# Where the up projection's first quad takes its weights from, and the y products of the SSD scan in one piece

## The chip, the cores and the metric

The kernel runs on one core of a Trainium2 chip. The metric is the device time of one execution in microseconds (us). All data are float32; most matrix products run in float32r, as three products of a high and a low part of each operand, so that the sum is close to float32.

## The reference

One decoder layer on 512 tokens of width 1024, cut to what the change touches:

```
h    = rms_norm(x) @ w_in                      # z, x/B/C, dt, q, k, v, f
y    = ssd_mixer(...)                          # 16 heads in 2 groups, chunks of 128 tokens
       y_diag = (C B^T * decay) @ (x dt)       # inside a chunk
       y_off  = (C exp(a_cs)) @ state          # from the chunks before it
       y      = rms_norm((y_diag + y_off + D x) * silu(z))   # per group of 512
x    = x + concat(y, fox_attention(...)) @ w_out
hf   = rms_norm(x)
u    = causal_conv3(hf @ w_up)                 # 1024 -> 5632, halves gate and value
out  = x + (silu(gate) * value) @ w_down       # 2816 -> 1024
```

## The kernel before, in words

**Splitting.** A weight block of 128 x 1024 comes by DMA into a raw tile, ScalarE (ACT) copies it into a float32r tile `wh`, VectorE (DVE) puts the rest `wl = raw - wh` into a second tile, and TensorE (PE) multiplies. `mm3` (line 110 is its matmul) issues the three products high by high, high by low, low by high for one block of 128 columns. Raw tiles `wraw` stand in a ring of three, the pairs `wh`, `wl` in another ring of three, beside a spare pair and, in the up stage, a far pair.

**Order.** A scheduler works out one static order for each engine, from the program's order, priorities (`urgent()`), explicit "issue after" edges and its own estimates of time. Each engine runs its order strictly: an instruction whose operand is late holds all behind it. Tiles of a pool are handed out in rotation as the scheduler places the work, so which of the three PSUM banks of a pool a sum gets also depends on the order.

**The SSD scan** (`ssd_scan`, two groups of eight heads) goes through four chunks of 128 tokens. For each, `side_by_side` issues 16 matmuls of 64 columns each as PE sees them (8 instructions in the order lists), two heads next to each other in the two column halves of the array: first the chunk's own product (`sc` by `x_tok`), then, from the second chunk on, the product with the state (`ce` by `state`) into the same bank `y`. Between the two, `norm_sum` puts one tiny matmul `ss`, the sum of squares of an earlier chunk. `x_tok` of the first chunk is filled by `to_tokens`, two heads at a time, as the projections that feed it come in: each pair of matmuls may start as soon as its two heads are there. PE meanwhile streams the 128 x 512 products of the projections (`g`, `pw`, `po`).

**The up projection** is done with one level of a Strassen-like scheme (seven products instead of eight) on eleven quads of four weight blocks, named B11, B12, B21, B22. Quad 0 is done plainly (`plain`): `weights` loads and splits its four blocks, `tokens(0)` multiplies with the first half of the tokens, `tokens(1)` with the second. Sums Z take B12 and B22, sums G take B11 and B21. Quad 0 starts while the last of the output projection (`po`, w7) and the second norm (`up_norm`, `up_turn`, transposes `hT`) are still running; the normed tokens stand in `uh` (high) and `ul` (low). All four raw blocks use the ring `wraw`, and B11 and B21 are split into the ring of three pairs, whose tiles the output projection's last weights still hold.

The later quads keep running sums of weight blocks: a tile `T` (named Ta, Tb; two of them in pool `ptt`, one in `pu`) receives a block, is split, and then another block is added into it by an accumulating DMA that GpSimd (POOL) issues (line 965, `more`). For quad 1 this is a chain of steps: n0's split, then an added block, n2's split, another added block, n3's split. SyncE (SP) issues the plain loads.

Of the kernel before, what the change touches and what calls it, by code (L numbers as in the profile page):

```python
# [8 lines left out]
F32 = mybir.dt.float32  # L9
F32R = mybir.dt.float32r  # L10
# [5 lines left out]
P = 128  # L16
# [17 lines left out]
LINE = 64  # L34
# [5 lines left out]
def tile_hybrid_layer(  # L40
# [18 lines left out]
    nc = tc.nc  # L59
# [329 lines left out]
    def ssd_proj(g):  # L389
        x_tok = [pss.tile([P, 512], F32, tag="x_tok", name="x_tok", bufs=7) for _ in range(NTB)]  # L390
        bT = pss.tile([P, SEQ], F32, tag="bT", name="bT", bufs=2)
        cT = pss.tile([P, SEQ], F32, tag="cT", name="cT", bufs=2)
        b_tok = pss.tile([P, NTB, P], F32, tag="b_tok", name="b_tok", bufs=2)
        gz = pss.tile([P, 4, SEQ], F32, tag="gz", name="gz", bufs=2)
        dx = pa.tile([P, 4, SEQ], F32, tag="v", name="dx", bufs=2)

        def to_tokens(j, src):
            t = obank("xT")
            for c in range(NTB):
                tc.keep_in_program_order(  # L400
                    pe.transpose(t[:, c * P : (c + 1) * P], src[:, c * P : (c + 1) * P], ident)
                )
            tv = t.rearrange("p (c f) -> p c f", c=NTB)
            if j < 8:
                jj = j - 4 * g
                for c in range(NTB):
                    for i in range(2):
                        h = 2 * jj + i
                        act.activation(
                            x_tok[c][:, h * HD : (h + 1) * HD], tv[:, c, i * HD : (i + 1) * HD], AF.Copy,  # L410
                            scale=tokS[:, 0, c, g * HPG + h : g * HPG + h + 1],
                        )
            else:
                act.copy(b_tok, tv)

        late = []
        for n, j in enumerate([8 + g, 10 + g] + list(range(4 * g, 4 * g + 4))):
            o = early.pop(j, None) or feature_tile(wxbc[j])
            if n > 3:
                to_tokens(*late.pop(0))  # L420
            xp = tmp("t", "xp")
            dve.tensor_mul(xp, o, R)
            dst = bT if j in (8, 9) else cT if j > 9 else tmp("t", "xs")
            cw = C_SCW + 4 * j
            act.activation(
                dst, xp, AF.Identity, scale=half_w[:, cw + 3 : cw + 4], bias=half_w[:, C_SCB + j : C_SCB + j + 1]
            )
            for s in range(1, 4):
                dve.scalar_tensor_tensor(
                    out=dst[:, s:], in0=xp[:, : SEQ - s], scalar=half_w[:, cw + 3 - s : cw + 4 - s], in1=dst[:, s:],  # L430
                    op0=ALU.mult, op1=ALU.add,
                )
            act.activation(xp, dst, AF.Tanh)
            dve.scalar_tensor_tensor(out=dst, in0=xp, scalar=1.0, in1=dst, op0=ALU.add, op1=ALU.mult)
            if j < 8:
                act.activation(dx[:, j - 4 * g, :], dst, AF.Copy, scale=pc[:, C_D + j : C_D + j + 1])
            if j < 10:
                late.append((j, dst))

        for j in range(4):  # L440
            o = feature_tile(wz[4 * g + j])
            if late:
                to_tokens(*late.pop(0))
            z = gz[:, j, :]
            th = tmp("t", "th")
            dve.tensor_mul(z, o, R)
            act.activation(th, z, AF.Tanh, scale=0.5)
            dve.scalar_tensor_tensor(out=z, in0=th, scalar=1.0, in1=z, op0=ALU.add, op1=ALU.mult)
        return x_tok, bT, cT, b_tok, gz, dx
# [4 lines left out]
    def per_head(ap):  # L454
        return ap[:, :, None].broadcast_to([P, HPG, HD])

    squares = []

    def norm_sum(after):
        g, c, t = squares.pop(0)  # L460
# [5 lines left out]
    def ssd_scan(g, x_tok, bT, cT, b_tok, gz, dx):  # L466
# [27 lines left out]
            dve.tensor_mul(sc, sc, cb[:, None, :P].broadcast_to([P, HPG, P]))  # L494
            return sc, ce, dte

        def side_by_side(o, w, m, start, stop):
            for j in range(4):
                for i, rows in ((1, HI), (0, LO)):
                    h = 2 * j + i  # L500
                    ins = pe.matmul(  # L501
                        o[rows, j * P : (j + 1) * P], w[:, h * HD : (h + 1) * HD], m[:, h, :],
                        start=start and j == 0, stop=stop and j == 3, skip_group_check=True,
                    )
                    if (j, i) != (0, 1):
                        tc.keep_in_program_order(ins)
            return ins

        def chunk(c, state, sc, ce, dte):
            s = slice(c * P, (c + 1) * P)  # L510
            o = mbank("y")
            own = side_by_side(o, x_tok[c], sc, True, c == 0)
            if c > 0:
                norm_sum(own)
                side_by_side(o, state, ce, False, True)
            if c < NTB - 1:
                xt = heads(x_tok[c])
                dve.tensor_mul(xt, xt, per_head(dte[:, 0, :]))
# [294 lines left out]
    def up_operand(n):  # L813
        return (oh[:, n], ol[:, n]) if n < 4 else (sh[:, n - 4], sl[:, n - 4])
# [126 lines left out]

    halfway, last_product, last_pool = [None], [None], [None]

    def product(w, n, o, part, first=False, last=True):
        h, l = w
        ah, al = up_operand(n) if n is not None else (gh, gl)
        for p in range(2):
            for k in range(4):
                c = slice(p * 512 + k * P, p * 512 + (k + 1) * P)
                ins = mm3(  # L950
                    o[:, p, part], h[:, c], l[:, c], ah[:, k], al[:, k], first and k == 0, last and k == 3, grouped=False
                )
            if p == 0:
                halfway[0] = ins
        last_product[0] = ins
# [309 lines left out]
    def spare():  # L1265
        return [pa.tile([P, 1024], F32R, tag=t, name=t, bufs=1) for t in ("wh", "wl")]

    def plain(q):
        u = quads[q]
        u.ws, u.halfway = [], []  # L1270

        def weights(quarter, where=None):
            r = wp.tile([P, 1024], F32, tag="wraw", name="wraw", bufs=3)
            nc.sync.dma_start(r, wup[quarter, q])
            u.ws.append(split_up(r, where))

        def tokens(half):
            for n, (name, rows) in enumerate((("Z", 0), ("Z", 1), ("G", 0), ("G", 1))):
                o = getattr(u, name)
                op = ((0, 1), (None, 2))[half][rows]  # L1280
                product(u.ws[n], op, o, (H1, H2)[half], rows == 0, rows == 1)
                u.halfway.append(halfway[0])

        return weights, tokens
# [15 lines left out]
    quads[0].Z = two_banks("Z", "Z")  # L1300
    sum_banks.close()
    up_banks["G"] = ctx.enter_context(tc.tile_pool(name="pq", bufs=2, space=PSUM, reuse_waits="tile"))
    weights(B11)
    with urgent():
        normed = up_norm(NTB - 1)
        act.activation(warm[:, 0:1], ss[:, NTB - 1 : NTB], AF.Silu)
# [14 lines left out]
    n2(1)  # L1321
    n5(1)
    four = [[wp.tile([P, 1024], F32R, tag=t, name=t, bufs=3) for t in ("wh", "wl")] for _ in range(3)]

    four.append([pu.tile([P, 1024 + LINE], F32R, tag=t, name=t)[:, LINE // 4 : 1024 + LINE // 4] for t in ("wh", "wl")])
    pairs.update(n2=four[0], n4=four[3], n1=four[1], n5=four[2])
    n0_weights(2)
    n3_weights(1)
# [297 lines left out]
```

## Time and profile before

| | us |
|---|---|
| runs (three) | 768.78, 770.18, 770.66 |
| median | 770.18 |
| profiled execution | 768.29 |
| its span | 766.5 |
| PE busy | 757.8 (99%) |
| DVE busy | 604.2 (79%) |
| ACT busy | 487.9 (64%) |

A row of the timeline has the start in us from the span's start, the duration in us, engine, source line, operation, output and inputs, shapes, the number of instructions merged, and in brackets the idle time before it and what ended it. Matmul rows overlap: a 128 x 512 product lasts 0.39 us and the next starts 0.23 us after it, so PE's pace is read from starts, and PE's idle time in brackets is shorter than the delay of the start.

### The profile page before, as it was taken

The page shows a single profiled execution, that of the slowest core. Times are in us where ns is not written, and L with a number is a line of the kernel's source. Part 1 is how long each engine was busy: PE and PEld are TensorE (multiplying, and loading weights), DVE is VectorE, ACT ScalarE, POOL GpSimd, SP SyncE. Part 2 cuts the span into 40 slices and gives each one's busy share as a digit, 9 for nine tenths or more (in the row PEclk, how much of TensorE's full clock was granted, in tenths as well). Part 3 has the DMA queues.
Part 4 walks back from the last instruction along what each step waited for, and adds up shares of the span by engine and source line. Part 5 has one row for each costly group of instructions (what it writes and reads, how often), then busy time and mean ns, then how long its engine had stood idle before and what let it go on. Part 6 is the DMA issues. An engine that isn't in the chain of part 4 may idle for free.

```text
span 766.5 us, 12541 instructions
## 1 busy us (share of the span) xinstructions
PE 757.8 (99%) x4647; PEld 650.8 (85%) x4647; DVE 604.2 (79%) x965; ACT 487.9 (64%) x870; POOL 200.7 (26%) x250
## 2 busy tenths in 40 slices
PE   9999999999999999999999999999999999999997
PEld 7888778787788778787777799999999999888786
DVE  5896789588568667488894887888888888998785
ACT  7655767664388667695673665766666666665461
POOL 0001013344253562235200001333333333213120
PEclk9999999999999999999999999999999999999999
DMA  9524223142154243334322317888888888589993
GB/s 342 181 99 143 90 103 132 62 138 90 49 192 128 65 152 96 111 126 123 83 83 83 110 56 150 198 195 195 195 193 195 193 195 192 152 236 209 240 192 99
DMA packets 35005, 112.39 MB, mean 147 GB/s; under 512 B 4160, under 2 KB 5248, under 8 KB 34944
## 3 DMA queue, kind: packets, MB, share of 16 engines
q1 hardware_dynamic: 24176, 74.89, 28.6%
q0 software_dynamic: 10336, 36.18, 26.1%
q8 instruction: 36, 0.59, 0.3%
q10 hardware_dynamic: 432, 0.52, 0.2%
q14 instruction: 25, 0.20, 0.1%
HBM read 105.71 MB, written 2.20 MB: 141 GB/s over the span
## 4 chain that ended last, share of the span: by engine, by line
PE 91%; issue 3%; DMA 2%; DVE 1%; POOL 1%; ACT 0%; SPq 0%; DVEq 0%; POOLq 0%; ACTq 0%
PE G L110 19%; PE pw L110 17%; PE g L110 13%; PE po L110 11%; PE Z L110 11%; PE Y L110 3%; PE o L681 2%; PE pT L671 2%; PE X L110 2%; PE y L501 2%; PE j L110 1%; PE S L648 1%; PE S L649 1%; POOL T L1204 1%; DMA T<-in_wdown_dram 1%
## 5 line engine op out<-in xcount | busy, mean ns | idle before, releaser
L110 PE MATMUL pw<-wh,xl 128*128 128x512 f32 x192 | 76.0, 396 | 0.0
L110 PE MATMUL pw<-wh,xh 128*128 128x512 f32 x192 | 75.8, 397 | 0.0
L110 PE MATMUL pw<-wl,xh 128*128 128x512 f32 x192 | 75.5, 393 | 0.0
L97 DVE TENSOR_TENSOR wl<-wraw,wh 128x1024 fp32r<-128x1024 f32 x51 | 64.0, 1255 | 13.1 <-ACT wh L96 12.7
L110 PE MATMUL G<-uh,wh 128*128 128x256 f32 x264 | 72.6, 277 | 0.9 <-DVE x L278 0.9
L110 PE MATMUL G<-ul,wh 128*128 128x256 f32 x264 | 72.5, 276 | 0.0
L110 PE MATMUL G<-uh,wl 128*128 128x256 f32 x264 | 71.6, 277 | 0.6 <-DVE wl L920 0.6
L96 ACT CAST wh<-wraw 128x1024 fp32r<-128x1024 f32 x51 | 53.5, 1051 | 19.0 <-PE pw L110 8.4
L110 PE MATMUL g<-xh,wl 128*128 128x512 f32 x144 | 56.8, 394 | 0.0
L110 PE MATMUL g<-xh,wh 128*128 128x512 f32 x144 | 56.8, 394 | 0.0
L110 PE MATMUL g<-xl,wh 128*128 128x512 f32 x144 | 56.7, 394 | 0.0
L965 POOL DMA_DIRECT2D Ta<-in_wup_dram x30 | 26.3, 875 | 113.1 <-DVE wl L920 113.1
L1215 ACT CAST wh<-T 128x1024 fp32r<-128x1024 f32 (+1 forms) x32 | 31.5, 985 | 33.4 <-DMA T<-in_wdown_dram 18.7
L920 DVE TENSOR_TENSOR wl<-Ta,wh 128x1024 fp32r<-128x1024 f32 x40 | 48.7, 1218 | 2.8 <-ACT wh L920 2.8
L110 PEld LDWEIGHTS G<-uh,wh 128*128 128x128 f32 x264 | 49.6, 188 | 1.3 <-ACT wh L920 1.3
L110 PEld LDWEIGHTS G<-ul,wh 128*128 128x128 f32 x264 | 49.6, 188 | 0.0
L110 PEld LDWEIGHTS G<-uh,wl 128*128 128x128 f32 x264 | 48.9, 188 | 0.8 <-DVE wl L920 0.8
L650 DVE CUSTOM_DVE_ANT_0 prob<-S,prob 128x128 f32<-128x128 f32 (+1 forms) x64 | 29.9, 486 | 23.8 <-PE S L649 22.1
L1215 DVE TENSOR_TENSOR wl<-T,wh 128x1024 fp32r<-128x1024 f32 (+1 forms) x32 | 36.4, 1137 | 13.4 <-ACT wh L1215 13.4
L920 ACT CAST wh<-Ta 128x1024 fp32r<-128x1024 f32 x40 | 42.1, 1053 | 6.3 <-DMA Ta<-in_wup_dram 4.3
L654 ACT ACTIVATE prob<-prob,nm 128x128 f32<-128x128 f32 (+1 forms) x64 | 35.7, 559 | 15.6 <-DVE nm L650 15.4
L110 PE MATMUL G<-sh,wh 128*128 128x256 f32 x160 | 44.2, 276 | 0.0
(296 smaller groups left out, 2415.4 us busy)
## 6 DMA issues: line engine op xcount, KB each, us to landing
Ta<-in_wup_dram POOLq DMA_DIRECT2D x30, 512.0 KB, 5.5
T<-in_wdown_dram POOLq DMA_DIRECT2D x20, 512.0 KB, 7.4
wraw<-in_wqk_dram SPq DMA_DIRECT2D x16, 512.0 KB, 3.4
wraw<-in_wout_dram SPq DMA_DIRECT2D x16, 512.0 KB, 3.3
wraw<-in_wup_dram SPq DMA_DIRECT2D x14, 512.0 KB, 4.9
wraw<-in_wxbc_dram SPq DMA_DIRECT2D x11, 512.0 KB, 3.3
Ta<-in_wup_dram SPq DMA_DIRECT2D x10, 512.0 KB, 7.0
Tb<-in_wup_dram SPq DMA_DIRECT2D x10, 512.0 KB, 6.4
```

The source lines that it names most:

```text
L96: act.copy(h, r)
L97: dve.tensor_tensor(out=l, in0=r, in1=raw(h), op=ALU.subtract)
L110: ins = pe.matmul(o, a, b, start=start and n == 0, stop=stop and n == 2, **kw)
L501: ins = pe.matmul(o[rows, j * P : (j + 1) * P], w[:, h * HD : (h + 1) * HD], m[:, h, :], start=start and j == 0, stop=stop and j == 3, ski ...
L648: pe.matmul(sps[:, :n], qst, ks[:, 0, :n], start=True, stop=False)
L650: dve.tensor_tensor_reduce(out=p, in0=sps[:, :n], in1=p, scale=-1.0, scalar=-NEG, op0=ALU.add, op1=ALU.min, accum_out=nm[:, qb : qb + 1],)
L654: act.activation(p, p, AF.Exp, scale=-1.0, bias=nm[:, qb : qb + 1], accum_out=sm[:, qb : qb + 1])
L671: pe.transpose(t[:, w : w + P], prob[:, o : o + P], ident)
L681: ins = pe.matmul(o[rows, kb * P :], v[:, kb, (2 * pair + i) % 8, :], pt[:, w : w + SEQ - kb * P], start=kb == 0, stop=kb == NTB - 1, skip ...
L920: ordered(act.copy(h, r), lambda: dve.tensor_tensor(out=l, in0=r, in1=raw(h), op=SUB))
L965: last_more[0] = nc.gpsimd.dma_start(t, wup[quarter, q], accum_op=ALU.add)
L1215: ordered(act.copy(hs, src[:, :n]), lambda: dve.tensor_tensor(out=ls, in0=src[:, :n], in1=raw(hs), op=SUB))
```

## The change

It has four parts.

1. The first matmul of the first chunk's own y product waits for the last of the copies into that chunk's `x_tok` (`copied[0]`); the others follow it in program order, as they did.
2. `norm_sum` stands behind the state's product instead of between the two y products.
3. Raw blocks B11 and B21 of quad 0 are loaded into the two `T` tiles of pool `ptt`, which hold the running sums of quads 2 and 3 later, at the time that `plain(0)` is set up. B11's split goes into the far pair in pool `pu` (the new `far_pair`, called a second time where the far pair was made before).
4. Quad 0's first G product, B11 with the first half of the tokens, runs through `low_last`: eight matmuls of high weights by high tokens, eight of low weights by high tokens, eight of high weights by low tokens.

```diff
                     for i in range(2):
                         h = 2 * jj + i
-                        act.activation(
+                        copied[c] = act.activation(
                             x_tok[c][:, h * HD : (h + 1) * HD], tv[:, c, i * HD : (i + 1) * HD], AF.Copy,
...
-        def side_by_side(o, w, m, start, stop):
+        def side_by_side(o, w, m, start, stop, whole=None):
...
                     if (j, i) != (0, 1):
                         tc.keep_in_program_order(ins)
+                    elif whole is not None:
+                        dep = mybir.DependencyInfo(mybir.DependencyClass.Sync, mybir.DependencyReason.DATA)
+                        tc.add_manual_dep(ins.ins, whole.ins.name, dep, reason="issue_after")
             return ins
...
-            own = side_by_side(o, x_tok[c], sc, True, c == 0)
+
+            side_by_side(o, x_tok[c], sc, True, c == 0, copied[c] if c == 0 else None)
             if c > 0:
-                norm_sum(own)
-                side_by_side(o, state, ce, False, True)
+                norm_sum(side_by_side(o, state, ce, False, True))
...
+    def low_last(w, n, o, part):
+
+        (h, l), (ah, al) = w, up_operand(n)
+        for a, b in ((h, ah), (l, ah), (h, al)):
+            for p in range(2):
+                for k in range(4):
+                    c = slice(p * 512 + k * P, p * 512 + (k + 1) * P)
+                    last_product[0] = halfway[0] = pe.matmul(
+                        o[:, p, part], a[:, c], b[:, k], start=a is h and b is ah and k == 0, stop=False, skip_group_check=True
+                    )
...
+    def far_pair():
+
+        return [pu.tile([P, 1024 + LINE], F32R, tag=t, name=t)[:, LINE // 4 : 1024 + LINE // 4] for t in ("wh", "wl")]
...
+        def load_rows(quarter, pool_, tag, bufs):
+            r = pool_.tile([P, 1024], F32, tag=tag, name=tag, bufs=bufs)
+            nc.sync.dma_start(r, wup[quarter, q])
+            return r
+
+        held = {n: load_rows(n, ptt, "T", 2) for n in (B11, B21)}
...
         def weights(quarter, where=None):
-            r = wp.tile([P, 1024], F32, tag="wraw", name="wraw", bufs=3)
-            nc.sync.dma_start(r, wup[quarter, q])
+            r = held[quarter] if quarter in held else load_rows(quarter, wp, "wraw", 3)
             u.ws.append(split_up(r, where))
...
-                product(u.ws[n], op, o, (H1, H2)[half], rows == 0, rows == 1)
+                if half == 0 and n == 2:
+                    low_last(u.ws[n], op, o, H1)
+                else:
+                    product(u.ws[n], op, o, (H1, H2)[half], rows == 0, rows == 1)
...
-    weights(B11)
+    weights(B11, far_pair())
...
-    four.append([pu.tile([P, 1024 + LINE], F32R, tag=t, name=t)[:, LINE // 4 : 1024 + LINE // 4] for t in ("wh", "wl")])
+    four.append(far_pair())
```

The change moves instructions on every engine, since the scheduler works out the order anew. Three places matter for what follows. Source lines of the changed kernel are up to 27 higher: the matmul of y is still line 501, the up split is 920 before and 923 now, `low_last` is 954.

**PE, the scan's second chunk of group 0**, where the two y products and the tiny `ss` stand in the stream of projections `g`. Before:

```order
L110 MATMUL g<-xh,wl 128x512
L501 MATMUL y<-sc,x_tok 64x128 x8
L463 MATMUL ss<-ones,yt 128x1
L501 MATMUL y<-ce,state 64x128 x8
L110 MATMUL g<-xh,wh 128x512
```

Now:

```order
L110 MATMUL g<-xl,wh 128x512
L501 MATMUL y<-sc,x_tok 64x128 x8
L501 MATMUL y<-ce,state 64x128 x8
L463 MATMUL ss<-ones,yt 128x1
L401 MATMUL xT<-ident,xs 128x128 x4
```

The two y products now follow each other in this chunk and in the five others that have a state; in the first chunk of group 0 the four separate pieces (`x2` each, with some 20 projections from one to the next) have become one `x8` where the last piece stood.

**PE and DVE at the start of quad 0**, with the semaphores that an instruction waits for. `x_85` is the residual, to which the output projection's sums `po` are added. PE before:

```order
L110 MATMUL po<-wh,mfl 128x512
L110 MATMUL G<-uh,wh 128x256 [waits DVE_49,Activation_49]
L110 MATMUL G<-ul,wh 128x256
L110 MATMUL G<-uh,wl 128x256 [waits DVE_49]
L110 MATMUL G<-uh,wh 128x256
```

PE now:

```order
L110 MATMUL po<-wh,mfl 128x512
L954 MATMUL G<-uh,wh 128x256 [waits DVE_49,Activation_49]
L954 MATMUL G<-uh,wh 128x256 x7
L954 MATMUL G<-uh,wl 128x256 x8
L954 MATMUL G<-ul,wh 128x256 [waits DVE_49]
L954 MATMUL G<-ul,wh 128x256 x7
L110 MATMUL G<-uh,wh 128x256 [waits Activation_49]
L110 MATMUL G<-ul,wh 128x256
L864 MATMUL hT<-ident,xw 128x128 [waits DVE_49,PE_49,Activation_49]
```

DVE before:

```order
L920 TENSOR_TENSOR wl<-wraw,wh 128x1024
L866 TENSOR_TENSOR ul<-one,uh 128x8x128
L278 TENSOR_TENSOR x_85<-po,x_85 128x512 x2
L866 TENSOR_TENSOR ul<-one,uh 128x8x128
L278 TENSOR_TENSOR x_85<-po,x_85 128x512
L125 TENSOR_SCALAR misc<-misc 128x1
L278 TENSOR_TENSOR x_85<-po,x_85 128x512
L920 TENSOR_TENSOR wl<-wraw,wh 128x1024
L849 SCALAR_TENSOR_TENSOR xw<-x_85,misc,nw 128x512 x2
```

DVE now:

```order
L923 TENSOR_TENSOR wl<-wraw,wh 128x1024
L923 TENSOR_TENSOR wl<-T,wh 128x1024
L278 TENSOR_TENSOR x_85<-po,x_85 128x512
L869 TENSOR_TENSOR ul<-one,uh 128x8x128
L278 TENSOR_TENSOR x_85<-po,x_85 128x512 x2
L869 TENSOR_TENSOR ul<-one,uh 128x8x128
L278 TENSOR_TENSOR x_85<-po,x_85 128x512
L125 TENSOR_SCALAR misc<-misc 128x1
L852 SCALAR_TENSOR_TENSOR xw<-x_85,misc,nw 128x512 x2
```

B11's low split has moved from behind the last addition to `x_85` to ahead of the last four, and the second `ul` has moved behind one more addition. On PE the wait for `wl` is gone, and one for `ul` has come, 16 matmuls later.

**ACT and PE in quad 1**, at the third and fourth split from Ta, with `z_4808` the kept sum that n5's product overwrites in Z. ACT before:

```order
L959 COPY y_4746<-G 128x512
L920 CAST wh<-Ta 128x1024
L959 COPY z_4808<-Z 128x512
L920 CAST wh<-Ta 128x1024
L1147 ACTIVATE ua<-ua 128x512 x2
```

ACT now:

```order
L973 COPY y_4746<-G 128x512
L923 CAST wh<-Ta 128x1024 x2
L973 COPY z_4808<-Z 128x512
L1161 ACTIVATE ua<-ua 128x512
L923 CAST wh<-Tb 128x1024
```

PE before, n5's product (Z) behind n1's (G, with `uh`), and n3's (G, with `sh`) only after the 24 of n5:

```order
L110 MATMUL G<-uh,wh 128x256
L110 MATMUL G<-ul,wh 128x256
L110 MATMUL G<-uh,wl 128x256
L110 MATMUL Z<-sh,wh 128x256
L110 MATMUL Z<-sl,wh 128x256
```

PE now:

```order
L110 MATMUL G<-uh,wl 128x256
L110 MATMUL G<-sh,wh 128x256
L110 MATMUL G<-sl,wh 128x256
L110 MATMUL Z<-sh,wh 128x256
L110 MATMUL Z<-sl,wh 128x256
```

The first two matmuls of n3 now stand ahead of n5's 24, and ACT's cast of n3's weights stands ahead of its copy of `z_4808`.

More of the change, by code (lines that the diff above doesn't have):

```diff
@@ L455, in per_head @@
         return ap[:, :, None].broadcast_to([P, HPG, HD])
-    squares = []
+    squares, copied = [], {}
     def norm_sum(after):
```

## The prediction

> **What bounds the kernel.** I read the page first (busy times, then the chain of work that ended last), then PE's waits, then PE's timeline at the places that the change touches.
>
> ```profile
> span 766.5 us, 12541 instructions
> PE 757.8 (99%) x4647; PEld 650.8 (85%) x4647; DVE 604.2 (79%) x965; ACT 487.9 (64%) x870; POOL 200.7 (26%) x250
> PE 91%; issue 3%; DMA 2%; DVE 1%; POOL 1%; ACT 0%; SPq 0%; DVEq 0%; POOLq 0%; ACTq 0%
> PE G L110 <- DVE x L278: 0.9, 1, 0.9
> PE G L110 <- DVE wl L920: 0.6, 1, 0.6
> ```
>
> PE is busy for 99% of the span and carries 91% of the chain. So there are two ways to gain: take out one of its few waits, or make its own stream shorter. The last two rows are the two waits at the start of quad 0, and no row of PE's waits names `y`: the scattered pieces never waited. What they cost must stand in PE's pace around them.
>
> **The change part by part.** *The four pieces of the first y product become one.* The first fence has the first piece, the second a whole product in group 1.
>
> ```profile
> 80.84 0.39 PE L110 MATMUL g<-xh,wh 128*128 128x512 f32 x1
> 81.16 0.44 PE L501 MATMUL y<-sc,x_tok 128*64 128x128 f32 x4
> 81.53 0.50 PE L110 MATMUL g<-xl,wh 128*128 128x512 f32 x1
> 81.87 0.39 PE L110 MATMUL g<-xh,wl 128*128 128x512 f32 x1
> ```
>
> ```profile
> 165.45 0.39 PE L110 MATMUL po<-wl,msh 128*128 128x512 f32 x1
> 165.68 0.39 PE L110 MATMUL po<-wh,msl 128*128 128x512 f32 x1
> 165.99 1.09 PE L501 MATMUL y<-sc,x_tok 128*64 128x128 f32 x16
> 167.02 0.50 PE L110 MATMUL po<-wh,msh 128*128 128x512 f32 x1
> 167.35 0.40 PE L110 MATMUL po<-wl,msh 128*128 128x512 f32 x1
> ```
>
> The undisturbed step of the stream is 165.68 - 165.45 = 0.23. From the last product before the piece to the second after it, 81.87 - 80.84 = 1.03; two steps would be 0.46, so a piece of 4 adds 0.57. The whole block adds 167.35 - 165.68 - 0.46 = 1.21. Four pieces at 0.57 make 2.28, one block 1.21: **-1.1**. The added wait for the last copy costs nothing where the block stands, at the old last piece, which needed that copy too and did not wait. Behind it in PE's queue are projections alone. If every piece had cost its share of a whole block, the gain would be 0; that is the lower end.
>
> *The tiny `ss` behind both y products, in six chunks.*
>
> ```profile
> 114.26 0.39 PE L110 MATMUL g<-xh,wl 128*128 128x512 f32 x1
> 114.58 1.09 PE L501 MATMUL y<-sc,x_tok 128*64 128x128 f32 x16
> 115.60 0.38 PE L463 MATMUL ss<-ones,yt 128*128 128x1 f32 x2
> 115.91 1.09 PE L501 MATMUL y<-ce,state 128*64 128x128 f32 x16
> 116.94 0.50 PE L110 MATMUL g<-xh,wh 128*128 128x512 f32 x1
> 117.27 0.40 PE L110 MATMUL g<-xl,wh 128*128 128x512 f32 x1
> ```
>
> ```profile
> 241.73 0.40 PE L110 MATMUL pw<-wh,xh 128*128 128x512 f32 x1
> 241.96 0.28 PE L463 MATMUL ss<-ones,yt 128*128 128x1 f32 x2
> 242.10 0.48 PE L110 MATMUL pw<-wl,xh 128*128 128x512 f32 x1
> 242.41 0.40 PE L110 MATMUL pw<-wh,xl 128*128 128x512 f32 x1
> ```
>
> Before, the group takes 117.27 - 114.26 = 3.01. After: 0.32 into the first y, 1.02 for it (114.58 to 115.60), the second y right behind. From the rows above, 12 more matmuls cost 1.21 - 0.57 = 0.64, so 16 more cost 0.85; I take 0.90. Then `ss`, and out of it 0.14 + 0.31 (241.96 to 242.41). The sum is 2.69, a gain of 0.32 a chunk. No row shows 32 y matmuls in one run. The other end: two whole blocks (1.21 each) and a lone `ss` (242.41 - 241.73 - 0.46 = 0.22) add 2.64 where the group before adds 3.01 - 0.46 = 2.55, a loss of 0.09. I take 0.32, since a run that goes on is what the 4 against 16 show: **-1.9** for six, between -1.9 and +0.5. The Trainium skill ("TensorEngine Tiling (Array Packing)", Key Properties) says that a change of tiling mode drains the array; y runs in tiles of 128 x 64, `ss` does not. By that rule each chunk loses two switches and the gain stands at its upper end; without it, at the lower. The rows above (0.37 for 4 matmuls, 1.03 for 16) side with the rule.
>
> Counted over the order lists, two other small groups on PE have also merged with neighbours, at about 0.2 each by the lone `ss`: **-0.4**, with 1 either way, since the whole mixer is ordered anew.
>
> *Quad 0's start.*
>
> ```profile
> 438.55 0.39 PE L110 MATMUL po<-wh,mfl 128*128 128x512 f32 x1
> 439.81 0.36 PE L110 MATMUL G<-uh,wh 128*128 128x256 f32 x1 [0.88 <-DVE x L278]
> 440.00 0.28 PE L110 MATMUL G<-ul,wh 128*128 128x256 f32 x1
> 440.85 0.39 PE L110 MATMUL G<-uh,wl 128*128 128x256 f32 x1 [0.57 <-DVE wl L920]
> ```
>
> ```profile
> 437.00 1.22 DVE L866 TENSOR_TENSOR ul<-one,uh 128x1024 fp32r<-128x1024 f32 x1
> 438.97 0.69 DVE L278 TENSOR_TENSOR x<-po,x 128x512 f32<-128x512 f32 x1
> 439.58 1.22 DVE L920 TENSOR_TENSOR wl<-wraw,wh 128x1024 fp32r<-128x1024 f32 x1
> 442.85 1.42 DVE L849 SCALAR_TENSOR_TENSOR xw<-x,misc,nw 128x512 f32<-128x512 f32 x2 [0.66 <-POOL misc L126]
> ```
>
> The second wait (0.57) is for B11's low split, which the third DVE row makes behind the last residual addition. It now stands ahead of four additions and has the far pair free, so **-0.6** (up to 0.7 by starts). The first wait (0.88) is for that last addition itself, at 438.97 + 0.69 = 439.66: G's bank was its bank. The change says nothing of banks, but the new order does: PE now waits for DVE a second time at `ul`, which stands *ahead* of the last addition; a first wait for the last addition would have covered it. So G has another bank and the 0.88 goes too: **-0.9**, or 0 if I misread it. What is late next: DVE has 1.22 more ahead, and one addition (about 0.6) more ahead of the second `ul`, which then ends near 437.00 + 1.22 + 1.22 + 0.6 = 440.0; PE needs it after 16 matmuls of 0.115 from 438.78, at 440.6. That holds. Then the transposes `hT` of the third token block need `xw`: by the same delay it starts about 0.6 later than before, near 441.3, and is half done (0.7) at 442.0, while PE is there after 26 matmuls, at 441.8: **+0.3** with the semaphore.
>
> *Quad 1.*
>
> ```profile
> 471.21 0.58 ACT L959 COPY z<-Z 128x512 f32<-128x512 f32 x1
> 472.78 1.05 ACT L920 CAST wh<-Ta 128x1024 fp32r<-128x1024 f32 x1 [1.00 <-DMA Ta<-in_wup_dram]
> ```
>
> ```profile
> 472.89 0.28 PE L110 MATMUL Z<-sh,wh 128*128 128x256 f32 x1
> 473.00 0.28 PE L110 MATMUL Z<-sl,wh 128*128 128x256 f32 x1
> ```
>
> Now n3's first two matmuls stand where Z<-sh stood, at 472.89, and need the cast that ends at 472.78 + 1.05 = 473.83. Both ends of this gap hang on PE's own earlier products (through n0's pair, its split and two accumulating transfers), so both move by the same amount and the gap stays: **+1.0**. Then Z<-sh needs the copy of `z_4808`, which has moved behind that cast: it ends near 473.74 + 0.58 = 474.32, PE is there at 473.88 + 0.23 = 474.11: **+0.25**. Between 0, if the transfers land a microsecond sooner, and the slower rival below.
>
> **The sum:** -1.1 - 1.9 - 0.4 - 0.6 - 0.9 + 0.3 + 1.25 = -3.35. On the profiled execution, 768.29 us, that is 764.9; the median of the three runs is 1.9 higher, so for the median, 770.18 - 3.3 = **766.9 us**. From quad 2 on, PE stays the bound and the shift is kept to the end.
>
> **The rivals.**
> *Covered wait in quad 1.* The two accumulating transfers land about 1 us earlier against PE than before. For it: a transfer takes from 3.6 to 8.2 us (below), so a microsecond is within their spread. Against: nothing makes them faster. Then -3.35 - 1.25 = -4.6, 765.6 us.
> *Bank.* G still waits for the last addition, which the extra split now pushes back by about 0.8, so quad 0 gains nothing (0.9 + 0.6 - 0.3 of gain fall away): -3.35 + 1.2 = -2.15, 768.0 us. For it: the row names that wait; against: the second wait for DVE.
> *y gains by the first product alone,* since `ss` between the blocks cost nothing: -3.35 + 1.9 = -1.4, 768.7 us. Against it, the 0.31 from `ss` to the next block.
> *Slower: the accumulating transfers collide with a load.*
>
> ```profile
> 461.78 16.26 SPq L969 DMA_DIRECT2D wraw<-in_wup_dram  x2
> DMA to landing us min/median/max: 3.6/5.5/8.2
> 467.67 0.28 PE L110 MATMUL Z<-uh,wl 128*128 128x256 f32 x1
> 465.75 1.23 DVE L920 TENSOR_TENSOR wl<-Ta,wh 128x1024 fp32r<-128x1024 f32 x1 [1.22 <-ACT wh L920]
> ```
>
> DVE's split of a `wraw` now follows n0's split at once instead of three short operations later, so the load that reuses that tile (461.78) starts some 1.8 us earlier in the first transfer's flight. If both transfers of the chain took the longest 8.2 instead of 5.5, n2's product, with a slack of 467.67 - 465.75 - 1.23 = 0.69, would be 2.0 late and n3's another 3.4 (0.7 and 2.7): +5.4, so -3.35 + 5.4 = +2.1, 772.3 us. It turns into a loss once the two together lose more than some 4 us. The Trainium skill ("DMA: Bandwidth & Descriptors", Issuing engines are not separate DMA queues) says that loads from any issuer run on the same 16 engines and interleave, so SP's load would take its time from POOL's transfer. But the load overlapped that transfer before as well, and 5.5 is the median with it.
>
> **How the numbers follow.** Forecast 0.50, covered wait 0.20, bank 0.12, y alone 0.11, collision 0.07. Two in ten are left out by 764.2 to 769.4: below it a covered wait with luck in the mixer's order, above it the collision and some of y alone. About 0.3% (2.3 us) can be told from no change: faster means below 767.9. Of the forecast 0.45, all of the covered wait and 0.03 of the bank case lie there, 0.68; within 0.3% are 0.25; slower is the collision, 0.07.
>
> **What would show it.** On PE's timeline: one y block of 16 near 97 to 99 us, six runs of 32, each `ss` behind, with 2.7 from the last product before to the second behind. The first G at 0.23 to 0.3 after the last `po`, no wait there for `x` or `wl`, a short one at `hT`. In quad 1 a wait of about 1 us on PE for ACT's `wh` from Ta and a small one for `z`. The prediction is wrong if the six y groups still take 3 us, if the wait for the residual addition is still there, or if PE waits in the attention stage, where it hardly did, eat what the scan gained.

## The result

The change made the kernel slower: 772.41 us against 770.15 (medians of 13 executions each), a ratio of 1.0057 with a 95% interval of 1.0033 to 1.0081. The means lie 4.1 us apart, more than the medians. The forecast was 766.9, faster. Eight of the 25 executions of the changed kernel that were timed in all (13 here, 12 in a later comparison) stand at 776.0 to 780.4 us, the other 17 at 769.6 to 774.0. No execution of the kernel before is above 772.02. The 17 by themselves are 1.8 above the kernel before in the mean. So one part of the loss is there without the long executions, and another part comes in the third that are long. Two executions further down, one of experiment 3 (1271.95 us) and one of experiment 6 (1542.6 us), were slow throughout, and no ratio counts them.

The page of the changed kernel, profiled in an execution of 771.72 us, answers to the three rows of the prediction's first fence:

```profile
span 770.0 us, 12537 instructions
PE 759.2 (99%) x4647; PEld 651.8 (85%) x4647; DVE 599.7 (78%) x965; ACT 489.2 (64%) x870; POOL 200.5 (26%) x250
PE 84%; issue 6%; DMA 5%; DVE 3%; POOL 1%; ACT 1%; SPq 0%; DVEq 0%; POOLq 0%; ACTq 0%
```

PE holds less of the chain, DMA and DVE more. The waits of PE that bear on the change (us in total, how often, the longest):

```profile
PE G L110 <- ACT wh L923: 1.5, 1, 1.5
PE X L110 <- DVE wl L1229: 1.3, 2, 0.8
PE Z L110 <- DVE wl L923: 0.8, 1, 0.8
PE X L110 <- ACT wh L1229: 0.7, 1, 0.7
PE Z L110 <- ACT wh L923: 0.2, 1, 0.2
```

Both waits of quad 0 are gone, as forecast. In their place stand one for `wh` at G and two at Z, all in quad 1, and more waits at X in the down stage than the one of 0.7 before.

To see where the time went I counted PE's matmuls in both traces, each at its median step, and compared the times at which the same sum of work was reached. The stretches are given in us of this sum, which runs 1 to 2 us behind the clock at 20 us and some 18 to 22 at the end. The last column has the three other profiles of the same order (experiments 1 and 10 below).

| stretch of work | forecast, us | first profile | the three others |
|---|---|---|---|
| the first 20 us | 0 | +0.83 | +0.53 to +1.50 |
| scan, to 270 us | -3.4 with the rest of the mixer | -2.91 | -2.90 to -2.91 |
| values of the second head pair (o), 270 to 280 | 0 | +2.68 | +2.67 to +2.68 |
| rest of attention and output projection | | -0.78 | -0.75 |
| quad 0, 425 to 440 | -1.2 | -1.75 | -1.74 to -1.77 |
| quad 1, 440 to 460 | +1.25 | +3.48 | +3.34 to +4.80 |
| down stage, from 680 | 0 | +1.88 | -0.70 to +0.40 |

The rows from the scan to quad 0 repeat within a few hundredths. Quad 1 and the down stage, which live on transfers, don't, and neither does the start. The first row isn't the change's: the profiled execution of the kernel before, at 768.29, is 1.9 under its median, and the profiles of experiments 3 and 11 with the mixer's old order also come 1.9 later to the first 20 us. The rows from the scan to quad 1 add up to +0.6 to +2.1 in the four profiles, where the forecast has -3.35.

**The scan** went as forecast. The first product stands in one block, and the two products of a later chunk follow each other, `ss` behind:

```profile
99.95 1.09 PE L501 MATMUL y<-sc,x_tok 128*64 128x128 f32 x16
...
113.94 0.39 PE L110 MATMUL g<-xl,wh 128*128 128x512 f32 x1
114.26 1.09 PE L501 MATMUL y<-sc,x_tok 128*64 128x128 f32 x16
115.19 1.04 PE L501 MATMUL y<-ce,state 128*64 128x128 f32 x16
116.16 0.38 PE L463 MATMUL ss<-ones,yt 128*128 128x1 f32 x2
```

The second product starts 0.93 after the first and takes 0.97, where 0.85 to 0.90 was assumed for 16 more.

**Attention** has what the forecast did not look for: no wait, but a dearer product. PE's timeline of the changed kernel, then of the kernel before, at the values' product of the second head pair:

```profile
281.19 1.07 PE L684 MATMUL o<-pt,v 128*64 128x512 f32 x2
282.20 0.33 PE L601 MATMUL qkT<-ident,tok 128*128 128x128 f32 x1
282.46 1.07 PE L684 MATMUL o<-pt,v 128*64 128x512 f32 x2
283.46 0.33 PE L601 MATMUL qkT<-ident,tok 128*128 128x128 f32 x1
283.72 0.86 PE L684 MATMUL o<-pt,v 128*64 128x384 f32 x2
284.51 0.33 PE L601 MATMUL qkT<-ident,tok 128*128 128x128 f32 x1
284.77 0.86 PE L684 MATMUL o<-pt,v 128*64 128x384 f32 x2
285.56 0.33 PE L601 MATMUL qkT<-ident,tok 128*128 128x128 f32 x1
285.82 0.87 PE L684 MATMUL o<-pt,v 128*64 128x256 f32 x8
```

```profile
284.54 2.38 PE L681 MATMUL o<-pt,v 128*64 128x512 f32 x16
286.84 0.50 PE L648 MATMUL S<-ks,qs 128*128 128x512 f32 x1
```

Before, the 16 matmuls of o take 2.30 from start to the next start. Now transposes `qkT` stand between its pieces. One head's 512 columns alone take 1.01 (281.19 to 282.20), and the other head's the same again. So each half of the array works by itself where the other head's matmuls are no longer next in the queue: in the whole block the 512 columns of both heads together take some 0.92 (512 of 1280, so 0.4 of 2.30). The four pieces of 512 and 384 columns take 1.01 + 1.00 + 0.79 + 0.79 = 3.59. In the whole block the same columns are 896 of 1280, so 0.7 of 2.30, or 1.61. That is 2.0 of the 2.68. The rest is put down to the switches from o to `qkT` and back; no row measures them by themselves. The Trainium skill ("TensorEngine Tiling (Array Packing)", Key Properties) says that tiles work independently and can run matmuls in parallel, and that a change of tiling mode drains the array; the first agrees with these rows (0.92 for both heads, 1.01 for one by itself), and the second would be the rest.

### The profile page after: what moved, and what is told of

Read it like the earlier page. It is cut to its first block, busy times and chain, and to the rows that moved or that the text cites. A ratio compares the mean times of both kernels' runs of the same rounds, so it can differ in the third digit from the quotient of the medians.

```text
span 770.0 us, 12537 instructions
## 1 busy us (share of the span) xinstructions
PE 759.2 (99%) x4647; PEld 651.8 (85%) x4647; DVE 599.7 (78%) x965; ACT 489.2 (64%) x870; POOL 200.5 (26%) x250
## 4 chain that ended last, share of the span: by engine, by line
PE 84%; issue 6%; DMA 5%; DVE 3%; POOL 1%; ACT 1%; SPq 0%; DVEq 0%; POOLq 0%; ACTq 0%
PE pw L110 17%; PE G L110 17%; PE g L110 13%; PE po L110 12%; PE Z L110 9%; PE o L684 3%; DMA T<-in_wdown_dram 2%; PE pT L674 2%; PE Y L110 2%; PE y L501 2%; DMA Ta<-in_wup_dram 2%; PE j L110 1%; PE S L652 1%; PE S L651 1%; POOL T L1218 1%
## 5 line engine op out<-in xcount | busy, mean ns | idle before, releaser
L110 PE MATMUL G<-uh,wh 128*128 128x256 f32 x256 | 70.3, 276 | 0.0
L110 PE MATMUL G<-ul,wh 128*128 128x256 f32 x256 | 70.3, 276 | 0.0
L110 PE MATMUL G<-uh,wl 128*128 128x256 f32 x256 | 69.2, 276 | 0.0
```

What stands on the lines that cost most here:

```text
L110: ins = pe.matmul(o, a, b, start=start and n == 0, stop=stop and n == 2, **kw)
```

## The experiments

The kernel before was timed beside each group on the same chip. Each ratio is to it.

**1. The changed kernel again**, unaltered, beside experiments 6 to 8.

> The changed kernel itself, unaltered, beside the next three on one chip. Theory A (every loss has a place): the same places as in the first profile, to the hundredth where no transfer is in play: from 20 to 280 us of work it gains 2.9 against the profile of before, loses 2.6 at the cut o, gains 1.9 at quad 0's start; in quad 1 it loses 2 to 5, by how long the first accumulated block takes (7.2 and 8.8 us in the two profiles of this order so far), and 0 to 2 in the down stage. Time against before: +0.2 to +0.6%. Theory B (chance alone): the loss in quad 1 is gone in this profile, and the time is within 0.1% of before.

1.0054 (1.0025 to 1.0084), median 771.91. The profile has the same places: scan -2.9, o +2.68, quad 0 -1.74, quad 1 +3.34. The down stage gives back 0.7 in this one, where the first lost 1.88. Over the four profiles of this order that stage goes from -0.7 to +1.9, and the order of every engine from quad 2 on is the one before. So the 1.9 us of the first profile can't be put down to the change. Theory A holds for all but the down stage.

**2. Parts 1 and 2 alone.** Of the diff, only the lines of `copied`, `side_by_side` and `chunk` are kept.

> Parts 1 and 2 alone (the y products of the scan); the up stage has the order it had before the change. Theory A (three places lose): the scan gains the 2.8 us that stand between the two profiles from 20 to 240 us, but the values' product o of one head pair, which the new order cuts into pieces with transposes qkT between them, loses 2.6 at 281 to 287 us, and the rest of the mixer gains 0.7, so 1 us faster than before at most, -0.9 by this sum, with the cut o to be seen in PE's timeline. The up stage then loses nothing. Theory B (the y parts are worth what the prediction said and all of the loss is in the up stage): -3.4 us.

0.9981 (0.9971 to 0.9992), -1.3 us in the medians. The profile shows o in the same pieces, at the same cost, and nothing lost in quads 0 and 1 beyond 0.1. Theory A's -0.9 lies inside the interval, theory B's -3.4 does not.

**3. Parts 3 and 4 alone**, the scan as before.

> Parts 3 and 4 alone (quad 0's weights and low_last); the scan and attention have the order they had before. Theory A: quad 0 gains 1.85, and quad 1 gives back 3.5 (1.45 at the second product, whose block lands late, and 2.0 where n3's first two matmuls stand ahead of n5's): +1.65 us, and up to +3.2 if the 1.5 us that PE waits in the down stage of the changed kernel come with it. Theory B (the loss of the changed kernel is chance, executions that happen to be slow): +0.05, that is -1.2 for quad 0 by the prediction and +1.25 for quad 1. If some executions stand 7 us above the others, as 4 of the 13 of the changed kernel do, their cause lies in the up stage.

1.0077 (1.0048 to 1.0106), from six executions: above the whole change, though the two intervals overlap. Quad 1 loses 3.4, as expected, but quad 0 gains only 0.2. PE's row, with DVE's ahead of it:

```profile
441.51 0.68 DVE L278 TENSOR_TENSOR x<-po,x 128x512 f32<-128x512 f32 x1
442.12 0.14 DVE L125 TENSOR_SCALAR misc<-misc 128x1 f32<-128x1 f32 x1
442.34 0.83 PE L951 MATMUL G<-uh,wh 128*128 128x256 f32 x5 [1.49 <-DVE misc L125]
```

PE waits 1.49 until the last residual addition is done at 441.51 + 0.68 = 442.19. (The row names the DVE operation that ended last. G starts 0.15 after the addition, as it does in the kernel before: 439.81 against 439.66.) This is the prediction's rival *bank*. G doesn't read that sum, so what is left to wait for is its bank: with the mixer's old order the banks seem to rotate so that G gets the bank of the last sum, which is inferred from the wait and not seen by itself. The added split ahead of the addition makes the wait longer than the 0.88 of before. One execution stands at 781.69.

**4. o in one block again.** The transposes of the fourth head pair stand behind the second pair's values:

```diff
-                with tc.issue_after(values_last[-1].ins) if pair == 4 else nullcontext():
+                with tc.issue_after(values_last[-1].ins) if pair in (3, 4) else nullcontext():
```

> The whole change, and the transposes qkT of the fourth head pair stand behind the last matmul of the second pair's o, so that o is one block of 16 again. Theory A: the five pieces of o with qkT between them (281.19 to 286.79) cost what pieces of y cost, by the excess over the pace of the stream; with the block whole the 2.6 us come back: -2.6 against the changed kernel on the same chip, all of it between 270 and 300 us. Rival (the 2.6 us are those of work that had to be done there anyway, and the delay moves to the projections behind): less than 0.5.

0.9989 (0.9981 to 0.9998), 769.12, or 2.8 below experiment 1 in the medians. PE's timeline:

```profile
281.06 2.37 PE L684 MATMUL o<-pt,v 128*64 128x512 f32 x16
283.36 0.77 PE L601 MATMUL qkT<-ident,tok 128*128 128x128 f32 x5
```

The block takes 2.30 again, and between 270 and 300 us PE is 2.7 earlier than in the changed kernel. Theory A holds on the place and the size. Its comparison with the pieces of y does not: those kept both halves of the array together, and cost only the switch.

**5. The first accumulated block of quad 1.** Two rows decide it. POOL issues the accumulating transfer, SP a plain load, and ACT's cast waits for the first. The kernel before, then the changed one:

```profile
459.13 0.95 POOL L965 DMA_DIRECT2D Ta<-in_wup_dram  x1 [16.31 <-DVE wl L920]
464.67 1.05 ACT L920 CAST wh<-Ta 128x1024 fp32r<-128x1024 f32 x1 [2.33 <-DMA Ta<-in_wup_dram]
```

```profile
457.47 0.95 POOL L979 DMA_DIRECT2D Ta<-in_wup_dram  x1 [14.54 <-issue]
458.03 0.33 SPq L983 DMA_DIRECT2D wraw<-in_wup_dram  x1
464.72 1.05 ACT L923 CAST wh<-Ta 128x1024 fp32r<-128x1024 f32 x1 [4.62 <-DMA Ta<-in_wup_dram]
```

From issue to cast it is 5.54 before, with the load 2.65 behind (461.78), and 7.25 now, with the load 0.56 behind. A first version held back the wrong load:

```diff
+        if (q, quarter) == (2, B21):
+            dep = mybir.DependencyInfo(mybir.DependencyClass.Sync, mybir.DependencyReason.DATA)
+            tc.add_manual_dep(ins.ins, first_more[0].ins.name, dep, reason="issue_after")
```

> The whole change, with one wait added: SP's load of B21 of quad 2 into the raw ring starts only when quad 1's first accumulated block has landed. In the changed kernel it starts at 458.03, 0.56 us after that accumulating transfer was issued, and the transfer takes 7.2 us (457.47 to 464.72) where it took 5.5 before. Theory A (the load slows the transfer): the block lands 5.5 us after its issue, near 463.0, PE's two waits in Z's first product of quad 1 (0.24 and 0.76) go, -1.4 us against the changed kernel. Rival (a transfer takes what it takes, 3.6 to 8.2 us, with or without the load): it still takes 7.2 and the waits stay, 0.

1.0018 (1.0005 to 1.0031). The load at 458.03 belongs to quad 3, not to quad 2, whose load comes some 20 us later. So the load stood where it stood (457.79), and the transfer took 8.8 (457.23 to 466.05). This run says nothing on the theory beside one more duration. The second version has `(3, B21)` in that line:

> The whole change, and the load that starts at 458.03 beside the first accumulating transfer (B21 of quad 3, not of quad 2) starts only when that transfer has landed. Theory A: the transfer, issued at about 457.3, lands after 5.5 us as in the profile of before, not after 7.2 or 8.8; Z's first product in quad 1 waits for nothing, -1.5 against the changed kernel on the same chip, more where the transfer took longest. Rival: the transfer takes 7 us or more without the load as well, and nothing is gained.

```profile
457.76 0.95 POOL L979 DMA_DIRECT2D Ta<-in_wup_dram  x1 [14.54 <-issue]
463.08 1.05 ACT L923 CAST wh<-Ta 128x1024 fp32r<-128x1024 f32 x1 [2.69 <-DMA Ta<-in_wup_dram]
463.13 0.33 SPq L984 DMA_DIRECT2D wraw<-in_wup_dram  x1
```

5.3 from issue to cast. Over all profiles: where the load starts within 0.6 of the transfer it takes 7.25 to 8.82 (eight profiles), and 5.32 to 5.54 where it starts 2.6 or more behind, or waits (seven profiles). Z's two waits are gone, and quad 1 loses 1.45 instead of 3.34. The ratio is 1.0003 (0.9979 to 1.0028), median 768.84. That is 3.1 below experiment 1, more than the expected 1.5; against the 3.34 to 4.80 that the four profiles of the changed kernel lose in quad 1, the 1.45 are 1.9 to 3.4 less. Two of its twelve executions stand near 776.8.

**6. Quad 1's order put back**, n3 behind n5 and its cast behind the copy of z:

```diff
-    n3_weights(1)
-    n3_product(1)
+    with tc.issue_after(z2_copy[0].ins):
+        n3_weights(1)
+    with tc.issue_after(last_product[0].ins):
+        n3_product(1)
```

> The whole change, with quad 1's order put back at one place: n3's first two matmuls stand behind n5's 24, and the cast of n3's weights behind the copy of z. Theory A: PE's wait of 1.47 for the cast and the 0.25 for the copy go, since the cast is ready (473.99) before n5's product ends (472.4 + 24 x 0.114 = 475.1): -1.9 us against the changed kernel, while the 1.45 at the second product stay. Rival (the wait only moves on to the next product, whose weights hang on the same chain of accumulated blocks): 0 to -0.5, with a new wait at n6's or n3's low split.

1.0013 (0.9997 to 1.003), median 770.91. The profiled execution is the one of 1542.6 us, so only the times speak: 0.7 below the changed kernel in the mean without the executions near 778 (770.8 against 771.5 in experiment 1), of which this run has none. The 1.9 expected isn't shown by this run alone. What it is worth is seen in the next.

**7. All three repairs together** (experiments 4, 6 and the second of 5).

> The whole change with the three repairs together: o whole, n3 behind n5 (and its cast behind the copy of z), quad 3's load behind the first accumulated block. Theory A: the scan's -2.9, quad 0's -1.9 and the rest of the mixer's -0.6 stay, nothing is lost in attention and quad 1; with 0 to 2 lost in the down stage that is -5.4 to -3.4 against before, a ratio of 0.993 to 0.9955. Rival (PE that is early in quad 1 only meets the same chain of transfers later, in the next quads): -2 or less, with new waits in quads 1 to 3.

0.9912 (0.9899 to 0.9926), 763.24: 6.7 us faster than the kernel before, and the fastest of all. All of PE's waits above 0.2:

```profile
PE X L110 <- DVE wl L1234: 1.6, 3, 0.8
PE g L219 <- DVE misc L141: 1.0, 1, 1.0
PE g L110 <- ACT wh L188: 0.7, 1, 0.7
PE po L110 <- DVE x L278: 0.3, 1, 0.3
```

No wait is left in the up stage, so the chain of transfers in quad 1 doesn't bind when nothing is put in its way. Against before, equal work is reached 2.9 earlier over the scan, 0.8 over the rest of the mixer, 1.7 over quad 0, and quad 1 gains 0.1, where with the load's repair alone it loses 1.45: the order is worth some 1.5 there. Together that is 5.5, the end of theory A's range. The time lies beyond that range (0.993 to 0.9955): its five executions stand between 762.1 and 764.9, and 1.2 of the 6.7 have no place in the profile.

**8. Part 1 alone**, `ss` between the products.

> Part 1 alone: the first chunk's own product in one block; ss stays between the two y products, the up stage as before. Theory A: the scan gains 1.1 (the pieces), o stays whole, nothing else moves: -1.1 against before, a ratio of 0.9985; the difference between this and the scan of the changed kernel is then what the move of ss is worth, 1.75 us over six chunks. Rival (ss between the blocks cost nothing, and the whole gain of the scan is the first block's): -2.9.

0.998 (0.9968 to 0.9992). In the profile the scan gains 1.18 (PE is 0.64 late at 20 us, as every profile is to some degree, and 0.54 early from 110 on), o is whole, and nothing else moves. So the first block is worth 1.2 and the move of `ss` 2.91 - 1.18 = 1.7. The cut of o comes only with part 2; part 2 without part 1 was not run.

**9. The whole change without `low_last`.**

```diff
-                if half == 0 and n == 2:
+                if False:
```

> The whole change without part 4: quad 0's first G product runs in the old form, a high, a low, a high product for each block, so that the low operand ul is wanted by the second matmul instead of the seventeenth. Theory A (low_last covers the second addition and the second ul): PE waits at the second matmul of G until ul is done, 438.0 + 1.2 - 437.2 or so, that is +1.0 to +1.9 at quad 0 against the changed kernel, and it comes later to quad 1 and loses that much less there, so +0 to +1 at the end. Rival (ul is there in any case): no wait, 0.

1.005 (1.0024 to 1.0076). PE's row and DVE's:

```profile
438.42 1.22 DVE L869 TENSOR_TENSOR ul<-one,uh 128x1024 fp32r<-128x1024 f32 x1
439.69 0.39 PE L110 MATMUL G<-ul,wh 128*128 128x256 f32 x1 [0.71 <-DVE ul L869]
```

Quad 0 gains 1.0 instead of 1.75: part 4 is worth 0.8 there, since it gives DVE the time of 16 matmuls. Quad 1 doesn't lose less for it, as theory A expected: it loses 4.6, with a first transfer of 8.5. The time at the end is that of the changed kernel within the interval. The profiled execution, 777.6 us long, is one of those near 778, and the last section draws on it.

**10. Two more profiles of the changed kernel**, for an execution near 778.

> The changed kernel once more, for one profile: 8 of its 25 executions so far stand at 776 to 780 us, above the rest at 769.6 to 774, and no profile has met one. If this one stands there, its trace shows one place more at which PE waits some 8 us or several transfers late at once; by theory A that place is in the up or the down stage, since the kernels with the up stage of before have no such execution in 12 and more. If it doesn't, quad 1 loses 2 to 5 us again.

> As the look before it: a second profile of the changed kernel, for the executions near 778 us. Theory A: a wait of some 8 us in the up or the down stage; rival: the same waits as in the other profiles and a slower pace all along.

772.19 and 770.47, neither near 778. They lose 4.7 and 4.8 in quad 1, with a first transfer of 8.7 and 8.8. So they speak for neither theory; the profile of experiment 9 does, and it sides with the rival, a slower pace (last section).

**11. Each half of the change with its own repair.** The y parts with o whole, and the up stage of before:

> Parts 1 and 2 alone with o kept whole; the up stage has the order of before. Theory A: the scan's -2.9 and the rest of the mixer's -0.7 stay, the cut o costs nothing, the up stage loses about 0.1 as in the y parts alone: -3.5 against before, a ratio of 0.9955. Rival (the up stage takes the gain back, because PE comes earlier to transfers that don't): -1 to -2.

0.9951 (0.9938 to 0.9964), 766.00. As theory A says: the scan and attention give 3.7, and the up stage takes nothing back.

The up parts with quad 1 repaired, and the mixer of before:

> Parts 3 and 4 alone with quad 1 repaired (n3 behind n5, its cast behind the copy of z, quad 3's load behind the first accumulated block); the mixer has the order of before. Theory A (quad 0's gain hangs on the bank that G gets, and so on the order of the mixer): G waits for the last residual addition as in the profile of the up parts alone, quad 0 gains 0.2 instead of 1.9, quad 1 loses nothing: -0.2 against before, 0.9997. Rival (the wait in that profile was chance, a late DVE): quad 0 gains 1.7 to 1.9, 0.9975.

0.9997 (0.9983 to 1.0011). G waits as in experiment 3:

```profile
442.30 1.17 PE L951 MATMUL G<-uh,wh 128*128 128x256 f32 x8 [1.49 <-DVE misc L125]
```

So the up parts by themselves are worth next to nothing (-0.3 in the profile). Their 1.7 in experiment 7 needs the bank that G gets from the mixer's new order. Together the halves make 0.9951 x 0.9997 = 0.9948. Of the 2.8 us from there to 0.9912 quad 0's bank explains 1.5 (1.73 against 0.2); the rest is not settled.

## Why the prediction was wrong, step by step

- *Four pieces, -1.1.* Right: 1.18 measured (experiment 8).
- *`ss` behind, -1.9.* Right in the mechanism: 1.7 by the difference of two profiles, near the upper end of the range.
- *Other small groups, "-0.4, with 1 either way, since the whole mixer is ordered anew".* **This is the first step that failed.** The term counted small groups and did not read where the large ones had gone. The new order cut o, at +2.68; against it stand 0.8 gained elsewhere. The scan's own rows gave the direction, that matmuls in half the array are dearer in small pieces (0.57 for 4, 1.21 for 16), but not the size: by those rows four more pieces cost some 1.4 (4 x (0.57 - 0.64/3)), an estimate, since no piece of y parts the two heads. PE's order in the profiles has o in twelve runs of instructions instead of eight.
- *Quad 0, -0.9 - 0.6 + 0.3.* Both waits went, 1.95 from the last `po` to G's own products, and 0.2 of it was given back up to the end of the quad, 0.1 of that at `hT`, where 0.3 was forecast. The reading that G's wait for the last addition goes was right for the whole change. Experiment 3 shows that it is no property of parts 3 and 4.
- *Quad 1, +1.0 + 0.25.* **The second step that failed.** n3 ahead of n5 was read rightly. PE's rows in the first profile:

```profile
472.31 0.28 PE L110 MATMUL G<-uh,wl 128*128 128x256 f32 x1
474.06 0.39 PE L110 MATMUL G<-sh,wh 128*128 128x256 f32 x1 [1.47 <-ACT wh L923]
474.28 0.28 PE L110 MATMUL G<-sl,wh 128*128 128x256 f32 x1
474.54 0.39 PE L110 MATMUL Z<-sh,wh 128*128 128x256 f32 x1
474.77 0.28 PE L110 MATMUL Z<-sl,wh 128*128 128x256 f32 x1
```

  It cost 2.0, not 1.25: G starts 1.64 late (472.42 to 474.06), Z 0.15 late (0.25 was forecast), and the step behind each of the two is 0.22 instead of 0.11. Ahead of it stands a loss of some 1.5 at Z's first product, which the sum has nothing of. The idea that both ends of the gap hang on PE's own products, "so both move by the same amount and the gap stays", missed that the chain of transfers was late by itself, because of the load beside the first.
- *The rival that accumulating transfers collide with a load,* held at 0.07, was the true one in quad 1. Its place and cause stand in the prediction: DVE's split follows at once, so the load starts earlier. The load came 2.1 nearer to the transfer (0.56 behind it instead of 2.65), close to the 1.8 worked out. What was mis-sized is the chance, and with it what the load does: it was argued that "the load overlapped that transfer before as well, and 5.5 is the median with it", but it overlapped only the second half, and 5.5 is the median of all 40 transfers into Ta, ten plain loads among them. Started beside it, the load makes the transfer 1.7 to 3.5 us longer. The rule of the Trainium skill quoted there ("DMA: Bandwidth & Descriptors", Issuing engines are not separate DMA queues), that the loads of all issuers run on the same engines, agrees with this. That the rival's 772.3 us stands so near the measured 772.41 is luck: it counts no loss in attention, and it lets the second transfer take 8.2 as well, which took 5.5.
- *"From quad 2 on, PE stays the bound and the shift is kept to the end."* True in the median of the profiles but not in each: the down stage moves by -0.7 to +1.9 with the same order. That belongs in the range.
- Not in the prediction at all: the slower pace that PE can fall into (below). If the one profile near 778 stands for all of them, a third of the executions get some 7.5 us from it (the distance of the means of the eight and the 17), more than half of the mean loss: (8 x 7.5) / 25 = 2.4 of some 4.1 us.

## What to carry to other kernels

When a change makes a scheduler work out the order anew, look in the new order for every group whose cost depends on its neighbours, half-array products first, and compare their number of runs before and after; a "small" reordering term can hold the largest loss. A load issued a few tenths of a microsecond behind a transfer that a chain waits for costs that chain some 2 to 3.5 us here, and one added wait on that load bought it back. A gain that comes from a bank or a buffer is the change's only as long as the rotation stays: measure each half alone before calling it the half's own.

## What the runs showed of the hardware

**Waits of PE can be followed by half its clock for 3.4 us.** Windows of the second profile of experiment 10 (start and end, length, busy us and instructions of each engine, PEclk, DMA share, GB/s), behind two waits of 1.77 and 0.76 us with two matmuls between them:

```profile
468.00:469.00 1.00, 0.65 (x5) 0.65 (x6) 1.00 (x3) 1.00 (x2) 0.28 (x1) 1.00 0.00 0
469.00:470.00 1.00, 1.00 (x8) 1.00 (x7) 1.00 (x2) 1.00 (x3) 0.59 (x1) 0.58 0.00 0
470.00:471.00 1.00, 1.00 (x6) 1.00 (x6) 1.00 (x2) 0.32 (x1) 0.00 (x0) 0.50 0.93 111
471.00:472.00 1.00, 1.00 (x7) 1.00 (x6) 0.96 (x2) 0.00 (x0) 0.80 (x1) 0.50 1.00 172
472.00:473.00 1.00, 1.00 (x8) 1.00 (x8) 0.79 (x2) 0.43 (x1) 0.07 (x1) 0.71 0.93 180
```

PE is busy again from 468.4, and yet the granted clock falls to 0.50 about 1 us later and stays for 3.4 us (0.84 of the window at 0.58, two whole ones, 0.58 of the one at 0.71). The matmuls step by 0.213 there instead of 0.113. Of five profiles with waits of 1.5 to 1.8 and 0.76 three show this, each for 3.4 us; of three with 0.2 to 0.4 and 0.76 none does. The Trainium skill ("TensorE: Matmul & The Clock Gate", What's actually happening) has a clock gate that halves the rate after an idle window of about 3.4 us, counted in free-running windows. The halving agrees, and its length is that of one window. That the waits need not fill 3.4 us, with some 2.5 of idling here, does not agree with a whole idle window. What parts the three profiles from the other two is open.

**PE has a second, slower pace at full clock.** Groups of PE between 480 and 640 us (busy us, mean ns of one), first in the changed kernel, then in the execution near 778 of experiment 9:

```profile
L110 PE MATMUL G<-ul,wh 128*128 128x256 f32 x198 | 54.3, 276 | 0.0
```

```profile
L110 PE MATMUL G<-ul,wh 128*128 128x256 f32 x191 | 53.3, 281 | 0.0
```

and windows of that execution (PE alone: busy us and instructions, PEclk, DMA share, GB/s):

```profile
480.00:520.00 40.00, 40.00 (x342) 1.00 0.86 190
520.00:560.00 40.00, 40.00 (x342) 1.00 0.82 186
```

The changed kernel does 355 or 356 matmuls in such a window of 40 us. The slow execution does 342, with the same instructions and the clock at 1.00, from the stall of quad 1 to the end of the up stage near 672 us: a step of 0.1178 instead of 0.1133. From 460 to 630 us of work it falls back by 6.7 us, about the distance of the executions near 778. The same slower step shows for 4 to 8 us behind the stall in three other profiles, and then ends; it also shows for some 10 us from 652 on in the profiles of both kernels, and, at 0.118 to 0.120, for 5 to 9 us between 449 and 464, ahead of any stall of quad 1, in every profile, that of the kernel before included. So the stream has a slower rhythm that mostly ends soon and sometimes lasts. It isn't the granted clock that tells the long executions: over the whole execution it is 0.996 to 1.000 in the eight, 0.994 to 1.000 in the 17. The kernels without a wait in the up stage behind quad 0 had no execution near 778. But neither had experiment 4 nor the first run of experiment 5 (23 executions with the full stall), nor experiment 6. That a stall sets off the lasting kind is therefore argued, not shown, and what ends it stays open.
